# Feed-forward of a decoder trunk: two-by-two block products in seven multiplications, in two phases

## The chip, the cores and the metric

One NeuronCore of a Trainium2 chip runs one program, an inference step of a small decoder trunk. The metric is the device time of that program in microseconds (us), lower is better. Engines: TensorE (PE in the rows, PEld for its weight loads), VectorE (DVE), ScalarE (ACT), GpSimd (POOL), and SyncE (SP), whose queue issues the DMAs.

## What is computed

Two layers over 1088 tokens (1024 of a prompt, 64 of eight samples), 1024 features, fp32 in and out. Each layer is a mixer (layer 0: gating and pooling; layer 1: sliding-window attention), a cross-attention into 256 memory tokens, and the feed-forward, which alone is changed:

```python
D_FF = 2816
def conv_ffn(h, g_ctx, w_up, conv_w, conv_b, w_down):      # h = rmsnorm(x)
    T = h.shape[1]
    up = h @ w_up                                          # (T, 1024) x (1024, 5632)
    g, u = up[..., :D_FF], up[..., D_FF:]
    g_ext = jnp.concatenate([g_ctx, g], 1)
    gc = conv_b
    for j in range(3):
        gc = gc + conv_w[j] * g_ext[:, j:j + T]            # causal, over tokens
    y = (gelu(gc) * u) @ w_down                            # (T, 2816) x (2816, 1024)
    return y, g_ext[:, -2:]                                # x += y
```

## The kernel before, in words

Activations lie feature-major: a tile has 128 features on its partitions and tokens along its columns. The tokens go in three chunks, `CHS`, of 384, 384 and 320 columns. Each fp32 operand is split exactly into two float32r parts, high and low, and each product is three matmuls into one PSUM accumulation (`mm3`, L222 to L225): high x high, high x low, low x high. The residual stream is held as such parts, `xh` and `xl`, for the whole program; so are three staging tiles (`stage`, L103) and five weight tiles (`wtile`, L106), so that weights of the next part of the program are loaded while the last one computes. TensorE's order is the order of the program text (`manual_schedule`); the other engines' queues, and SyncE's, are put in an order by the scheduler, and each works in order.

`mem(l)` (L674) is the cross-attention. Its last part multiplies with `m_w_o` chunk by chunk and calls `x_update` (L267): VectorE adds PSUM to `xh`, GpSimd adds `xl`, and `split_x` (L254) splits the sum again and adds its square to `acc`, from which `norm_chunk` makes the RMS factors of each token and `spread` (L315) puts them along the columns (`rv`).

`ffn(l, last)` (L914) runs over 22 blocks `hb` of 128 hidden features. `gu(hb)` loads and splits a gate and an up weight of 1024 x 128 (`load_cols`, the gain folded in by GpSimd, L195; high part by ScalarE, L197; low part by GpSimd, L198). Per chunk: `proj_fm`, 8 x 3 matmuls for the gate (L227); VectorE times `rv` (L945); the convolution as one ScalarE and two VectorE operations (L956 to L958); GELU (L961); GpSimd times `rv` (L966); 24 matmuls for up; VectorE product (L968); split of the result into `h` (L296, L297). `down(i)` takes two blocks: for each of eight output blocks and each chunk six matmuls (L985) and one VectorE add from PSUM onto the running residual `x32` (L992). Up and down alternate: `gu(2i)`, `down(i-1)`, `gu(2i+1)`. In the last `down` of layer 0 each finished block is split again into `xh`/`xl` at once; in the last `down` of layer 1 each finished chunk is transposed and stored (`final`, L1000).

## Time and profile before

| | |
|---|---|
| median of 3 runs | 2722.21 us (2721.33 to 2723.23) |
| span of the profiled execution | 2719.6 us |
| TensorE busy | 2652.5 us, 98% of the span |
| VectorE busy | 1642.5 us, 60% |
| ScalarE busy | 915.0 us, 34% |
| GpSimd busy | 1062.7 us, 39% |
| mean granted TensorE clock | 0.987 of full |

The page of a profile lists the busy time of each engine, the span in slices, the DMA queues, the chain of work that ended last, and groups of equal instructions. Further views answer for a stretch: busy time by engine in windows, instructions in order of time, waits. Matmul durations are pipelined: a row's 0.33 us is the time from issue to the last result, and what a matmul costs in a stream is the distance between two starts.

### The profile page before, as it was taken

To read this page: it belongs to the slowest core of one execution; us is meant where nothing else is said; L and a number is where in the kernel's file an instruction comes from. 1 tells how busy PE (TensorE), PEld (TensorE's weight loads), DVE (VectorE), ACT (ScalarE), POOL (GpSimd) and SP (SyncE) were. 2 spreads that over 40 slices of the span, in tenths; PEclk is the share of its full clock that TensorE was granted. 3 is DMA by queue.
4 is the path that set the end of the run, shared out by engine and by line. 5 is a ranking of instruction groups with operands and counts; after the bars stand their busy time and mean duration, and the time that the engine had idled before them with its cause. 6 is when DMAs were issued, how large, how long until landed. Compare 5 with 4: busy or idle time off the path is not lost.

```text
span 2719.6 us, 39268 instructions
## 1 busy us (share of the span) xinstructions
PE 2652.5 (98%) x15552; PEld 2469.7 (91%) x15552; DVE 1642.5 (60%) x3286; ACT 915.0 (34%) x1903; POOL 1062.7 (39%) x748
## 2 busy tenths in 40 slices
PE   8999999999999999999999989999999999999999
PEld 6998887899999999999876768877999999999999
DVE  8646965766555555554667677856665545555544
ACT  5224544332222222221545555553322222222221
POOL 3516533655333333331533333424663333333420
PEclk9999999999999999999999998999999999999999
DMA  8302102311111111110111021113111111111101
GB/s 268 113 11 69 47 32 86 101 47 40 47 40 47 47 47 47 40 47 24 58 37 46 1 63 47 47 40 117 55 39 47 47 47 47 47 40 47 47 24 69
DMA packets 167798, 150.49 MB, mean 55 GB/s; under 512 B 6465, under 2 KB 132511, under 8 KB 167614
## 3 DMA queue, kind: packets, MB, share of 16 engines
q1 hardware_dynamic: 167614, 147.98, 17.6%
q8 instruction: 122, 2.00, 0.3%
q14 instruction: 62, 0.51, 0.1%
HBM read 136.06 MB, written 11.82 MB: 54 GB/s over the span
## 4 chain that ended last, share of the span: by engine, by line
PE 83%; DVE 9%; POOL 2%; ACT 2%; issue 2%; DMA 0%; SPq 0%; ACTq 0%; DVEq 0%; POOLq 0%
PE psa L223 18%; PE psa L224 18%; PE psa L225 18%; PE psb L223 6%; PE psb L225 6%; PE psb L224 6%; DVE s L297 3%; PE psb L128 2%; PE psb L746 1%; PE psb L771 1%; PE psb L807 1%; DVE xl L257 1%; DVE w L219 1%; PE psa L128 1%; PE psa L1202 1%
## 5 line engine op out<-in xcount | busy, mean ns | idle before, releaser
L223 PE MATMUL psa<-xh,w 128*128 128x384 f32 (+1 forms) x2304 | 752.8, 327 | 5.1 <-DVE gp L945 5.1
L225 PE MATMUL psa<-xh,w 128*128 128x384 f32 (+1 forms) x2304 | 751.6, 326 | 0.0
L224 PE MATMUL psa<-xl,w 128*128 128x384 f32 (+1 forms) x2304 | 751.1, 326 | 0.0
L198 POOL TENSOR_TENSOR w<-st,w 128x1024 fp32r<-128x1024 f32 x140 | 343.2, 2454 | 419.4 <-ACT w L197 411.4
L223 PEld LDWEIGHTS psa<-xh,w 128*128 128x128 f32 x2304 | 433.0, 188 | 6.2 <-DVE gp L945 5.7
L224 PEld LDWEIGHTS psa<-xl,w 128*128 128x128 f32 x2304 | 433.1, 188 | 0.0
L225 PEld LDWEIGHTS psa<-xh,w 128*128 128x128 f32 x2304 | 432.9, 188 | 0.0
L223 PE MATMUL psb<-h,w 128*128 128x384 f32 (+1 forms) x1056 | 348.6, 330 | 2.6 <-DVE x L992 2.5
L225 PE MATMUL psb<-h,w 128*128 128x384 f32 (+1 forms) x1056 | 347.1, 329 | 0.0
L224 PE MATMUL psb<-h,w 128*128 128x384 f32 (+1 forms) x1056 | 346.9, 329 | 0.0
L197 ACT ACTIVATE w<-st 128x1024 fp32r<-128x1024 f32 x164 | 172.8, 1057 | 503.6 <-PE psb L225 362.8
L992 DVE TENSOR_TENSOR x<-psb,x 128x384 f32<-128x384 f32 (+1 forms) x480 | 251.1, 532 | 148.4 <-PE psb L225 147.0
L966 POOL TENSOR_TENSOR t<-t,rv 128x384 f32<-128x384 f32 x132 | 127.6, 966 | 353.7 <-ACT t L961 284.6
L195 POOL TENSOR_TENSOR st<-st,vec 128x1024 f32<-128x1024 f32 x84 | 166.1, 1977 | 205.8 <-DMA st<-in_f_w_up_dram 135.3
L968 DVE TENSOR_TENSOR t<-t,psa 128x384 f32<-128x384 f32 x132 | 70.1, 531 | 239.2 <-POOL t L966 239.2
L224 PE MATMUL psa<-s,w 128*128 128x384 f32 (+1 forms) x576 | 197.5, 343 | 16.5 <-DVE s L297 15.8
L223 PE MATMUL psa<-s,w 128*128 128x384 f32 (+1 forms) x576 | 197.8, 343 | 6.1 <-ACT s L296 6.0
L223 PEld LDWEIGHTS psb<-h,w 128*128 128x128 f32 x1056 | 198.2, 188 | 5.3 <-DVE x L992 5.0
L225 PEld LDWEIGHTS psb<-h,w 128*128 128x128 f32 x1056 | 198.3, 188 | 0.0
L224 PEld LDWEIGHTS psb<-h,w 128*128 128x128 f32 x1056 | 198.3, 188 | 0.0
L225 PE MATMUL psa<-s,w 128*128 128x384 f32 (+1 forms) x576 | 194.1, 337 | 0.0
L223 PE MATMUL psa<-w,xh 128*128 128x512 f32 (+1 forms) x432 | 180.1, 417 | 0.0
(289 smaller groups left out, 4332.9 us busy)
## 6 DMA issues: line engine op xcount, KB each, us to landing
st<-in_f_w_up_dram SPq DMA_DIRECT2D x88, 512.0 KB
st<-in_f_w_down_dram SPq DMA_DIRECT2D x44, 512.0 KB
ks<-in_m_w_kv_dram SPq DMA_DIRECT2D x16, 512.0 KB
st<-in_cache_mem_k_dram SPq DMA_DIRECT2D x16, 512.0 KB
k<-in_cache_mem_v_dram SPq DMA_DIRECT2D x16, 512.0 KB
st<-in_ab_w_in_dram SPq DMA_DIRECT2D x12, 512.0 KB
st<-in_c_w_qkv_dram SPq DMA_DIRECT2D x12, 512.0 KB
ks<-in_x_prompt_dram SPq DMA_DIRECT2D x8, 512.0 KB
```

The lines of the kernel that those rows point to most:

```text
L128: T.transpose(out, in_, idt[:rows, :rows])
L195: (eng or P).tensor_tensor(out=v, in0=v, in1=gain.unsqueeze(2).to_broadcast([128, shape[0], shape[1]]), op=ALU.mult)
L197: S.activation(w[:, 0, :], st, AF.Copy)
L198: (eng or P).tensor_tensor(out=w[:, 1, :], in0=st, in1=f(w[:, 0, :]), op=ALU.subtract)
L219: V.scalar_tensor_tensor(out=w[:, 1, k, :], in0=sk, scalar=gk, in1=f(w[:, 0, k, :]), op0=ALU.mult, op1=ALU.subtract)
L223: mm(out, lhsT=ah, rhs=bh, start=first, stop=False)
L224: mm(out, lhsT=ah, rhs=bl, start=False, stop=False)
L225: mm(out, lhsT=al, rhs=bh, start=False, stop=last)
L297: V.tensor_tensor(out=t[:, 1, :src_n], in0=src, in1=f(t[:, 0, :src_n]), op=ALU.subtract)
L966: P.tensor_tensor(out=ge[:, :n], in0=ge[:, :n], in1=rv[c], op=ALU.mult)
L968: V.tensor_tensor(out=ge[:, :n], in0=ge[:, :n], in1=pu[:, :n], op=ALU.mult)
L992: V.tensor_tensor(out=xm, in0=ps[:, :n], in1=xm, op=ALU.add)
```

## The change

The feed-forward's products are made as two-by-two block products with seven multiplications in place of eight (the form with shared sums, in which the second, third and fourth results build on partial sums of the first). The tokens go in two halves of 544 (`HT`), each half in two quarters of 272 (`QT`); the weights go in blocks of 256 output features and two halves of the inner dimension.

- `combos_w` loads two weight pieces and makes seven left operands, four of them from sums on GpSimd; ScalarE and VectorE split each into two parts. `combos_b` makes seven right operands of a token half, sums and low parts all on VectorE.
- `seven` walks over jobs. A job is seven products of 3 x `nk` matmuls of 272 columns; its order is 1, 7 of the job before, 5, 6, 4 of the job before, 2, 3. Products 6, 7 and 4 go on accumulating in the bank of product 1, product 3 in that of product 5, and each partial result is read out in between.
- All of up comes first. The right operands `B` of both token halves are made at the start, from the normalised residual, and stay. The gated rows go to DRAM (`hd`). Then all of down, in segments of 6, 6, 6 and 4 blocks: rows are read back, combined (`load_b`), and each of the seven results of a job is added to `x32`.
- The residual leaves the chip at the end of `mem` (`xq` in DRAM) and is read back into `x32` for down. `xh`, `xl`, `stage`, `wtile` and `tmp` are no longer held over the feed-forward: their pools are closed and opened again behind it, and the residual is split anew (`after_ffn`). The last tiles are transposed and stored behind the last job (`final`).

The diff, cut to its core:

```diff
-    def x_update(c, m, ps):
+    def x_update(c, m, ps, xq=None):
...
-        split_x(c, m, t1)
+        if xq is None:
+            split_x(c, m, t1)
+            return
+        squares(c, m, t1)
+        o = CHS[c][0]
+        for q in range(2):
+            a, b = max(o, HT * q), min(o + n, HT * q + HT)
+            if a < b:
+                nc.sync.dma_start(out=xq[q][:, m, a - HT * q:b - HT * q], in_=t1[:, a - o:b - o])
...
+    def seven(jobs):
...
+            pa_ = psA()
+            prod(job, pa_, "1", True)
+            out("m1", pa_[:, :QT])
+            last("7")
+            pc_ = psB()
+            prod(job, pc_, "5", True)
+            out("m5", pc_[:, :QT])
+            prod(job, pa_, "6", False)
+            out("u2", pa_[:, :QT])
+            last("4")
+            pb_ = psB()
+            prod(job, pb_, "2", True)
+            out("m2", pb_[:, :QT])
+            prod(job, pc_, "3", False)
+            out("m53", pc_[:, :QT])
...
+    def combos_w(pl, src1, src2, nk, engs):
...
+        def split(i, src):
+            t = pl.tile([128, 2, nk, 128], F32R, tag="w", name="w", bufs=R["wbufs"])
+            S.activation(t[:, 0], src, AF.Copy)
+            engs[i].tensor_tensor(out=t[:, 1], in0=src, in1=f(t[:, 0]), op=ALU.subtract)
+            w[i] = t
...
+        split("1", a11)
+        s1 = comb(a21, a22, ALU.add)
+        split("5", s1)
+        s2 = comb(s1, a11, ALU.subtract)
+        split("6", s2)
+        split("2", a12)
+        split("3", comb(a12, s2, ALU.subtract))
+        split("7", comb(a11, a21, ALU.subtract))
+        split("4", a22)
...
+    def combos_b(pl, tl, x, j0, nj, b, engs):
...
+            S.activation(t[:, 0, j0:j0 + nj], src, AF.Copy)
+            engs[i].tensor_tensor(out=t[:, 1, j0:j0 + nj], in0=src, in1=f(t[:, 0, j0:j0 + nj]), op=ALU.subtract)
...
+        split("1", x11)
+        t1 = comb(x12, x11)
+        split("5", t1)
+        t2 = comb(x22, t1)
+        split("6", t2)
+        split("2", x21)
+        split("3", x22)
+        comb(x22, x12, x12)
+        split("7", x12)
+        split("4", comb(x21, t2))
...
+    def ffn(l, last, xq, rvq, rs):
...
+            R["wbufs"] = 10
+            wpl = es.enter_context(pool(f"fw{l}"))
+            bq = es.enter_context(pool(f"fb{l}"))
+            B = [{i: bq.tile([128, 2, 4, QT], F32R, name=f"b{q}{i}") for i in "1562374"} for q in range(2)]
+            with ExitStack() as ee:
+                ep = ee.enter_context(pool(f"fe{l}"))
+                for q in range(2):
+                    for j in range(0, 4, 2):
+                        hx = ep.tile([128, 2, 2, HT], F32, tag="hx", name="hx")
+                        for kh in range(2):
+                            nc.sync.dma_start(out=hx[:, kh], in_=xq[q][:, 4 * kh + j:4 * kh + j + 2, :])
+                        for kh in range(2):
+                            for i in range(2):
+                                kb = 4 * kh + j + i
+                                V.scalar_tensor_tensor(out=hx[:, kh, i], in0=hx[:, kh, i], scalar=g_ffn[l][:, kb:kb + 1],
+                                                       in1=rvq[:, HT * q:HT * q + HT], op0=ALU.mult, op1=ALU.mult)
+                        combos_b(None, ep, hx, j, 2, B[q], ident)
...
+            def load_b(s, q):
+                nk = SEGS[s] // 2
+                hx = ep.tile([128, 2, nk, HT], F32, tag="hx", name="hx")
+                for kh in range(2):
+                    nc.sync.dma_start(out=hx[:, kh], in_=hd[s][:, kh, :, HT * q:HT * q + HT])
+                b = {i: bq.tile([128, 2, nk, QT], F32R, tag="b", name="b", bufs=14) for i in "1562374"}
+                combos_b(None, ep, hx, 0, nk, b, ident)
+                return b
...
+            def down_out(mp, q):
+                def add(i, nh, ps):
+                    x = x32[q][:, 2 * mp + i, QT * nh:QT * nh + QT]
+                    V.tensor_tensor(out=x, in0=ps, in1=x, op=ALU.add)
...
-        mix0(mem_kv())
-        mem(0)
-        ffn(0, False)
-        swa()
-        mem(1)
-        ffn(1, True)
+        with ExitStack() as rs:
+            with ExitStack() as es:
+                open_main(es, 0)
+                mix0(mem_kv())
+                xq, rvq = mem(0, rs)
+            x32, conv_out = ffn(0, False, xq, rvq, rs)
+            with ExitStack() as es:
+                open_main(es, 1)
+                after_ffn(0, x32, conv_out)
+                rs.close()
+                swa()
+                xq, rvq = mem(1, rs)
+            x32, conv_out = ffn(1, True, xq, rvq, rs)
+            final(x32, conv_out)
```

Readout of a result: in a gate job of up, ScalarE copies three partial results and VectorE makes three sums, then the convolution runs over 544 columns; in an up job VectorE makes the sums, GpSimd (VectorE for one of four) multiplies with the gate, and SyncE's queue stores the rows.

## Rows read from the trace of the kernel before

**Rows 1.** The page: busy time, share of the span and instructions of each engine.

```profile
PE 2652.5 (98%) x15552; PEld 2469.7 (91%) x15552; DVE 1642.5 (60%) x3286; ACT 915.0 (34%) x1903; POOL 1062.7 (39%) x748
```

**Rows 2.** Windows of both feed-forwards and the tail: busy us, granted clock, DMA share, GB/s.

```profile
523.90:1321.50 797.60, 792.26 (x4782) 788.50 (x4782) 447.50 (x801) 202.53 (x340) 319.38 (x211) 1.00 0.15 44
1912.30:2711.80 799.50, 796.34 (x4831) 795.27 (x4831) 434.75 (x785) 184.07 (x298) 299.11 (x193) 1.00 0.15 45
2711.80:2719.60 7.80, 2.66 (x24) 2.33 (x22) 2.56 (x4) 1.78 (x3) 0.00 (x0) 1.00 0.50 173
```

**Rows 3.** The same view, a stretch in the middle of layer 0's feed-forward.

```profile
700.00:900.00 200.00, 200.00 (x1214) 199.96 (x1213) 106.50 (x194) 46.92 (x77) 73.26 (x44) 1.00 0.15 45
```

**Rows 4.** Timeline, TensorE: start, duration, instruction; widths 384 and 320.

```profile
800.17 0.33 PE L223 MATMUL psa<-xh,w 128*128 128x384 f32 x1
...
801.03 0.33 PE L225 MATMUL psa<-xh,w 128*128 128x384 f32 x1
...
2708.70 0.31 PE L224 MATMUL psb<-h,w 128*128 128x320 f32 x1
...
2709.29 0.31 PE L225 MATMUL psb<-h,w 128*128 128x320 f32 x1
```

**Rows 5.** Timeline, weight loads of six matmuls with two columns each.

```profile
516.03 0.78 PEld L283 LDWEIGHTS psb<-ones,acc 128*128 128x128 f32 x6
```

**Rows 6.** Chain that ended last (a load of 0.5 MB), and windows of 10 to 20 us.

```profile
1373.83 3.69 DMA st<-in_c_w_qkv_dram
...
10.00:20.00 10.00, 10.00 (x42) 8.36 (x42) 9.46 (x18) 7.26 (x13) 1.55 (x2) 1.00 1.03 391
```

**Rows 7.** Timeline, VectorE's convolution steps without a wait for GpSimd.

```profile
807.04 0.62 DVE L958 SCALAR_TENSOR_TENSOR t<-gp,vec,t 128x384 f32<-128x384 f32 x1
...
816.73 0.57 DVE L958 SCALAR_TENSOR_TENSOR t<-gp,vec,t 128x336 f32<-128x336 f32 x1
```

**Rows 8.** Timeline, VectorE, instructions that follow each other.

```profile
812.72 0.42 DVE L948 TENSOR_TENSOR gp<-psa,rv 128x256 f32<-128x256 f32 x1 [1.68 <-PE psa L225]
813.06 0.21 DVE L951 TENSOR_TENSOR gp<-psa,rv 128x64 f32<-128x64 f32 x1
...
1320.60 0.54 DVE L257 TENSOR_TENSOR xl<-x,xh 128x384 fp32r<-128x384 f32 x1
1321.06 0.55 DVE L265 TENSOR_TENSOR acc<-acc,t 128x384 f32<-128x384 f32 x1
1321.53 0.48 DVE L992 TENSOR_TENSOR x<-psb,x 128x320 f32<-128x320 f32 x1
1321.93 0.83 DVE L257 TENSOR_TENSOR xl<-x,xh 128x384 fp32r<-128x384 f32 x1
```

**Rows 9.** Windows around an idle stretch of TensorE.

```profile
1891.20:1893.40 2.20, 0.14 (x2) 0.04 (x1) 1.59 (x4) 1.39 (x4) 2.20 (x3) 1.00 0.00 0
1893.80:1900.40 6.60, 5.32 (x20) 5.28 (x21) 4.20 (x7) 1.84 (x6) 2.28 (x3) 0.50 0.01 4
```

**Rows 10.** Groups by line and form: GpSimd and ScalarE; busy, mean ns | idle before.

```profile
L966 POOL TENSOR_TENSOR t<-t,rv 128x384 f32<-128x384 f32 x88 | 88.9, 1010 | 284.6 <-ACT t L961 284.6
L966 POOL TENSOR_TENSOR t<-t,rv 128x320 f32<-128x320 f32 x44 | 38.7, 879 | 69.0 <-ACT t L964 69.0
L296 ACT ACTIVATE h<-t 128x384 fp32r<-128x384 f32 x88 | 46.2, 525 | 201.4 <-DVE t L968 201.4
```

**Rows 11.** Timeline, VectorE and GpSimd at the same time.

```profile
814.43 2.26 DVE L957 SCALAR_TENSOR_TENSOR t<-gp,vec,t 128x336 f32<-128x336 f32 x1 [0.94 <-ACT t L956]
819.35 0.55 DVE L992 TENSOR_TENSOR x<-psb,x 128x384 f32<-128x384 f32 x1
...
813.92 2.41 POOL L198 TENSOR_TENSOR w<-st,w 128x1024 fp32r<-128x1024 f32 x1 [4.62 <-ACT w L197]
818.98 2.41 POOL L198 TENSOR_TENSOR w<-st,w 128x1024 fp32r<-128x1024 f32 x1
```

**Rows 12.** Timeline, TensorE at the end: the transposes of the last chunk.

```profile
2711.64 2.82 PE L128 MATMUL psb<-idt,x 128*128 128x128 f32 x24
```

More of the change, by code (lines that the diff above doesn't have):

```diff
@@ L23 @@
 NT = 9
+HT = 544
+QT = 272
+SEGS = [6, 6, 6, 4]
 NEG = -1.0e30
@@ L893, in mem @@
                     norm_chunk(j // 2 - 1)
+                    factors(j // 2 - 1)
                 if hf == 0 and c:
```

415 lines of the change are left out of this document (284 added, 131 removed).

## Prediction

> **What bounds the kernel now.** I read the page's busy times first: TensorE is busy 98% of the span, VectorE 60%, ScalarE 34%, GpSimd 39% [rows 1]. Then the stretches of the two feed-forwards: layer 0 from 523.9 to 1321.5 us, layer 1 from 1912.3 to 2711.8 us and a tail of 7.8 us to the span's end, 1604.9 us in all, with TensorE without a hole in the middle [rows 2, 3]. The reader is to see that nothing but TensorE's stream sets the time there. Third, the timeline, for what one matmul takes: five starts of 384 columns take 0.86 us, four of 320 columns 0.59 us [rows 4], 0.172 and 0.147 us each. Over the stretch of 200 us, 1214 matmuls of mean width 362.7 came, one per 0.1647 us [rows 3]. At the full clock (2.4 GHz) a column is 0.417 ns, so 384 columns are 0.160 us and 320 are 0.133: about 13 ns come on top of each matmul at either width.
>
> The Trainium skill, TensorE: Matmul & The Clock Gate, section "Back-to-back issue gap", gives N/2.4 + 2.5 ns when the clock is high. The trace does not agree: by that rule 384 columns would start every 162.5 ns and not every 0.17 us. By it the new matmul of 272 columns would take an estimated 115.8 ns, the matmuls of a layer 642 us, and the whole some 2627 us.
>
> **What the change does to TensorE.** Before, a layer has 44 x 3 x 24 = 3168 up matmuls and 11 x 8 x 3 x 2 x 3 = 1584 down matmuls, 4752, which at 0.1643 us (two of 384 at 0.173, which the mean over 200 us wants, to one of 320 at 0.147) are 781 us. After, a job is seven products of 3 nk matmuls of 272 columns: 44 up jobs with nk = 4 (3696 matmuls), 24 down jobs with nk = 3 and 8 with nk = 2 (1848), 5544 in all. One takes 113.3 + 13.2 = 126.5 ns, extrapolated from the two widths. Bounds: below, the weight loads, six of which go in 0.78 us with 0.19 us for the last, 0.118 us apart [rows 5]; above, the 320-column start, 0.147 us. I take 126.5 because two widths gave the same constant. That is 467.5 us up and 233.8 us down, 701.3 us: 79.5 us less per layer, 159 us in two. The question is what of it is given back.
>
> **Start of the up phase.** Before, the up matmuls take the next chunk at once. After, TensorE needs all seven right-hand combinations of a token half, and these are made from one tile `hx` with a single buffer, in four rounds (two halves, two k parts). By the shapes and the order of opening of the pools, `hx` lies some 185 to 194 KiB up, on the last `s3` tiles of mem(), which the last mem matmul reads (E): so it can't be loaded earlier. A round is
> - two loads, 1.11 MB: 3.7 us for the first half MB and 1.4 us for the rest at 391 GB/s, 5 us [rows 6];
> - four scalar_tensor_tensor of 544 columns, 0.70 us apart from 0.62 us at 384 and 0.57 at 336 [rows 7]: 2.8 us;
> - eleven VectorE operations of 544 columns. From start to start 384 columns take 0.46 to 0.47 us, and PSUM reads of 256 and 320 columns 0.34 and 0.40 us [rows 8]: 1.03 ns a column and 0.07 us, so 0.63 us here, 7.0 us.
>
> So 14.8 us a round, and the first combination of the second round is there after 5 + 2.8 + 1.4 = 9.2 us. With 2 us for the last residual and the issue, the first matmul starts at E + 26. Its first five products take 7.6 us, to E + 33.6; the second half's first product is ready at E + 2 + 3 x 14.8 + 9.2 = E + 55.6. Idle: 26 + 22 = 48 us a layer (bounds 36, where loads and the VectorE work overlap, and 65, where SyncE's queue puts residual stores and weights ahead of `hx`). The norm's matmuls and the weights' splits fit into these holes.
>
> After a hole the granted clock is at the lower level: 0.50, 1.2 GHz, over 6.6 us behind the nearly idle 2.2 us at 1891 us [rows 9]. At most half of such 6.6 us is lost each time; I take 2.5 us, three holes a layer, 7.5 us (0 to 10).
>
> **The up phase.** Per pair of blocks TensorE has 4 x 84 x 0.1265 = 42.5 us. VectorE: 14 splits of 512 columns at 0.60 (8.4 us), eight conv steps of 544 with the wait for the one before at 0.82 (6.6), evictions 5, small copies 2: 22 us. GpSimd: eight sums of 512 columns (1.26 us, between 0.88 at 320 and 1.01 at 384 and on with their slope of 2 ns a column) and six products at 0.78: 14.8 us [rows 10]. ScalarE: 14 splits at 0.63, 14 copies out of PSUM at 0.4 and 8 passes of the conv at 0.7 to 0.9: 21 us, scaled from 0.525 us at 384 [rows 10]. All below 42.5. What can hurt is the order: a bank is accumulated on again two products (3 us) after its copy was due, and VectorE and ScalarE work in order. VectorE with two SBUF inputs waits for a running GpSimd operation: 0.57 us of work took 2.26 us and ended 0.4 us behind GpSimd's, while an add from PSUM ran beside one in 0.55 us [rows 7, 11]. Stalls: 10 us a layer (0 to 40). The new stores of gated rows (1088 B a partition, four per up job) go through SyncE's queue, nearly free (DMA share 0.15 [rows 3]).
>
> **Down.** Per segment of six blocks TensorE has 8 x 63 x 0.1265 = 63.8 us. VectorE: 56 adds of 272 at 0.35 (19.5 us, one per product, where before one add closed six matmuls), 28 weight splits of 384 at 0.467 (13.1), 22 operations of 816 columns on the gated rows at 0.91 (20.0): 52.6 us. GpSimd: 16 sums of 384, 1.0 us each [rows 10]. About half of VectorE's time is of the kind that waits; with 0.4 us for each sum it is at 59 us, 93% of TensorE's. In the last segment (four blocks) it is 43 + 4 against 42.5 us, so above it. In that state, with two products (2.3 us) of slack, I take 18 us of stalls a layer (5 to 45).
>
> Its start: `hx` of this phase lies on right-hand tiles that the last up job still reads, so the first product begins some 7 us after up's end; then VectorE has, for three jobs, 20 us of combinations, 6.5 of weights, 7.3 of adds and 3 of waiting, 37 us against 24 on TensorE. Loss 7 + 13 = 20 us (12 to 30). The residual's 4.5 MB load (11.4 us at that rate) comes at the same time.
>
> **Ends.** Layer 0: splitting the residual again was interleaved with the last down group and now follows it, but the first token half is final two jobs earlier: 5 us. Layer 1: nine tiles are transposed and stored behind the last job, where before only the last chunk's 24 transposes (2.82 us) and its stores stood there [rows 12]. 4.5 MB at 391 GB/s are 11.4 us, with 2.5 us ahead and 2 us behind: 16 us. mem()'s updates lose a copy and a subtraction: -1 us a layer.
>
> **Sum.** Layer 0: 48 + 7.5 + 467.5 + 10 + 20 + 233.8 + 18 + 5 = 809.8 us, before 797.6. Layer 1: with 16 for 5, 820.8 us, before 799.5 + 7.8 = 807.3. Together +25.7, less 2 for mem(): +24 us. The profiled execution has a span of 2719.6 us, the median of the runs is 2722.2, so 2746 us.
>
> **Rivals.**
> 1. Faster: the engines keep up, and only the holes remain. Start 42 + 5, up stalls 3, down's start 14, down stalls 8, ends 5 and 14: 778 and 787 us, 40 us less than before: 2681. For it: every engine's sum is below TensorE's in up and in the large segments. Against: the last segment's sum isn't, and 1.14 us per down product leaves no room for two 816-column operations in a row.
> 2. Slower by the shared port: VectorE's down phase sets the end. If each GpSimd sum holds VectorE for its whole length, a segment takes 52.6 + 16 = 68.6 us and the last one 55: 261 us, with in-order waits 274, and up's stalls grow to 25: 37 us more a layer, 2820. It decides as soon as more than 0.7 us of each 1.0 us sum blocks VectorE in down. For it: the row of 2.26 us. Against: adds from PSUM run beside GpSimd, and are half of the instructions [rows 11]. The Trainium skill, SBUF — State Buffer, section "SBUF: two separate sides", says just this: VectorE with two SBUF inputs against a GpSimd operation is an exclusive lock for the whole instruction. By that rule the time is this rival's; the trace agrees for single instructions and cannot show how often they meet.
> 3. The matmul is cheaper or dearer than 126.5 ns: at 118 ns, the weight load's, 654 us of matmuls a layer and 2652 in all; at 147 ns 815 us and some 2970. Two widths on one line speak against both.
>
> **How the numbers follow.** A measurement tells about 0.2% (5.4 us) from no change. Forecast 0.37 for 2728 to 2790; between it and rival 1, within 5.4 us of before, 0.10; rival 1 0.33; rival 2 0.17; rival 3 0.03 (0.02 below, 0.01 above). So faster 0.35, same 0.10, slower 0.55. The range 2665 to 2825 takes in the forecast, most of rivals 1 and 2 and no more.
>
> **What would show it.** Right: TensorE starts 0.126 to 0.127 us apart in mid-phase; two holes of 20 to 28 us at each start of up, VectorE busy in them; in down VectorE over 85% and TensorE waiting for its adds. Wrong: the second half's hole missing (then `hx` does not serialize), starts at 0.12 or 0.147, or GpSimd at the head of VectorE's waits over all of up. The least sure terms are the holes and the down stalls; if either is half of what I took, the sign turns.

## The result, and the profile after

The changed kernel takes 2822.3 us (median of 4 runs, 2818.13 to 2824.95), the kernel before 2721.8 beside it: ratio 1.037, 95% interval 1.0355 to 1.0385. The profiled execution has a span of 2823.2 us, 103.6 more than before. The prediction said 2746: the sign was right, the loss was four times as large.

The page of the changed kernel: busy time, share and instructions of each engine, and the granted clock in 40 slices, in tenths of 2.4 GHz. It answers [rows 1].

```profile
PE 2534.6 (90%) x17136; PEld 2336.3 (83%) x17136; DVE 1899.0 (67%) x3798; ACT 1190.9 (42%) x2483; POOL 983.5 (35%) x856
...
PEclk9999999779999997999899988999599999989999
```

TensorE has 118 us less to do and waits for 289 us instead of 67. Where it waits, windows of the changed kernel say: up and down of layer 0, the 11 us behind it, up and down of layer 1, the tail. Columns as in [rows 2]: TensorE, weight loads, VectorE, ScalarE, GpSimd, clock, DMA share, GB/s.

```profile
533.90:1066.00 532.10, 475.94 (x3709) 473.30 (x3708) 329.58 (x618) 230.23 (x427) 198.93 (x182) 0.94 0.24 76
1066.00:1357.10 291.10, 250.25 (x1854) 245.99 (x1853) 238.81 (x425) 97.57 (x169) 70.60 (x64) 0.91 0.29 100
1357.10:1368.10 11.00, 0.35 (x4) 0.09 (x2) 7.30 (x10) 11.00 (x28) 10.14 (x14) 0.57 0.50 161
1981.00:2515.80 534.80, 476.69 (x3709) 474.03 (x3708) 333.33 (x618) 230.05 (x427) 196.89 (x182) 0.93 0.24 76
2515.80:2805.20 289.40, 247.81 (x1852) 243.43 (x1852) 239.12 (x424) 97.47 (x168) 71.79 (x64) 0.92 0.29 100
2805.20:2823.20 18.00, 9.19 (x76) 7.99 (x74) 8.26 (x27) 5.86 (x10) 0.00 (x0) 0.90 0.70 260
```

The middle of up, the same 200 us as [rows 3]:

```profile
700.00:900.00 200.00, 200.00 (x1588) 200.00 (x1588) 121.48 (x235) 90.12 (x170) 81.57 (x78) 1.00 0.25 81
```

Three matmuls of 272 columns there, in the timeline, which answer [rows 4]:

```profile
700.08 0.29 PE L964 MATMUL psb<-b,w 128*128 128x272 f32 x1
700.21 0.29 PE L962 MATMUL psb<-b,w 128*128 128x272 f32 x1
700.34 0.29 PE L963 MATMUL psb<-b,w 128*128 128x272 f32 x1
```

200 us by 1588 is 125.9 ns a matmul, against 126.5 in the prediction, and TensorE waits for nothing there. The rule that the prediction cited from the Trainium skill (TensorE: Matmul & The Clock Gate, "Back-to-back issue gap"), which that section gives for a matmul by itself and not for a stream with weight loads, makes an estimated 115.8 ns; the trace doesn't agree.

So the gain on TensorE is there, and the loss lies at the joints. From the starts of the 5544 matmuls of 272 columns of a layer I read how long each stretch took, and by how much each job was longer than its matmuls (counted off as 84 a job in up, 63 or 42 in down):

| stretch, us | predicted, layer 0 / 1 | measured, layer 0 / 1 |
|---|---|---|
| end of mem(), against before | -1 / -1 | +10.0 / +9.0 |
| last product of mem() to the end of up | 533 / 533 | 532.3 / 534.9 |
| up's last to down's first product | 7 / 7 | 9.0 / 9.0 |
| first four jobs of down, over their matmuls | 13 / 13 | 24.5 / 25 |
| three segment boundaries of down | 18 / 18 | 24.8 / 22.7 |
| behind the feed-forward (layer 0: against before; layer 1: the whole tail, 7.8 before) | 5 / 16 | 24.3 / 18.3 |

The 24.3 us are read at the 800th matmul behind down's last: 179.3 us after it, against 155.0 in the kernel before. Up came out as forecast; the terms around it did not. What TensorE waited for longest (whole span; us, times, longest):

```profile
PE psa L962 <- ACT m L1152: 59.5, 2, 30.7
PE psa L962 <- DVE x L1253: 50.0, 24, 5.8
PE psa L962 <- ACT b L1037: 23.7, 2, 11.9
PE psb L344 <- DVE dg L343: 18.3, 12, 3.7
```

### The profile page after: what moved, and what is told of

The parts are those of the page before. It is cut to its first block, busy times and chain, and to the rows that moved or that the text cites. A ratio compares the mean times of both kernels' runs of the same rounds, so it can differ in the third digit from the quotient of the medians.

```text
span 2823.2 us, 45209 instructions
## 1 busy us (share of the span) xinstructions
PE 2534.6 (90%) x17136; PEld 2336.3 (83%) x17136; DVE 1899.0 (67%) x3798; ACT 1190.9 (42%) x2483; POOL 983.5 (35%) x856
## 3 DMA queue, kind: packets, MB, share of 16 engines
q1 hardware_dynamic: 183358, 223.76, 24.3%
## 5 line engine op out<-in xcount | busy, mean ns | idle before, releaser
L962 PE MATMUL psa<-b,w 128*128 128x272 f32 x2112 | 623.2, 295 | 152.1 <-ACT m L1152 59.5
L964 PE MATMUL psa<-b,w 128*128 128x272 f32 x2112 | 619.1, 293 | 10.2 <-DVE w L1011 10.2
L963 PE MATMUL psa<-b,w 128*128 128x272 f32 x2112 | 618.4, 293 | 10.1 <-DVE b L1038 10.1
L962 PEld LDWEIGHTS psa<-b,w 128*128 128x128 f32 x2112 | 406.1, 192 | 160.7 <-ACT m L1152 60.2
L964 PE MATMUL psb<-b,w 128*128 128x272 f32 x1584 | 462.8, 292 | 8.6 <-DVE w L1011 8.6
L963 PE MATMUL psb<-b,w 128*128 128x272 f32 x1584 | 463.4, 293 | 2.5 <-DVE b L1038 2.5
L962 PE MATMUL psb<-b,w 128*128 128x272 f32 x1584 | 463.7, 293 | 0.0
L964 PEld LDWEIGHTS psa<-b,w 128*128 128x128 f32 x2112 | 406.2, 192 | 12.1 <-DVE w L1011 11.9
L963 PEld LDWEIGHTS psa<-b,w 128*128 128x128 f32 x2112 | 406.1, 192 | 10.7 <-DVE b L1038 10.7
L1016 POOL TENSOR_TENSOR sc<-st 128x512 f32<-128x512 f32 (+2 forms) x152 | 196.0, 1289 | 474.7 <-DMA st<-in_f_w_up_dram 202.3
L1011 DVE TENSOR_TENSOR w<-sc,w 128x512 fp32r<-128x512 f32 (+2 forms) x304 | 221.0, 728 | 151.4 <-ACT w L1010 150.8
L964 PEld LDWEIGHTS psb<-b,w 128*128 128x128 f32 x1584 | 304.2, 192 | 9.2 <-DVE w L1011 9.2
L963 PEld LDWEIGHTS psb<-b,w 128*128 128x128 f32 x1584 | 304.3, 192 | 3.1 <-DVE b L1038 3.1
L962 PEld LDWEIGHTS psb<-b,w 128*128 128x128 f32 x1584 | 305.1, 193 | 0.2
L1010 ACT ACTIVATE w<-sc 128x512 fp32r<-128x512 f32 (+2 forms) x304 | 173.4, 571 | 209.0 <-PE psa L964 144.0
L1010 ACT ACTIVATE w<-st 128x512 fp32r<-128x512 f32 (+2 forms) x228 | 130.0, 573 | 148.8 <-PE psb L964 107.3
L232 PE MATMUL psa<-w,xh 128*128 128x512 f32 (+1 forms) x432 | 180.8, 419 | 10.6 <-ACT w L227 10.6
L1011 DVE TENSOR_TENSOR w<-st,w 128x512 fp32r<-128x512 f32 (+2 forms) x228 | 167.6, 737 | 25.7 <-ACT w L1010 25.3
L1016 POOL TENSOR_TENSOR sc<-st,sc 128x512 f32<-128x512 f32 (+2 forms) x76 | 91.8, 1208 | 264.4 <-DVE w L1011 261.6
```

Source lines behind the costliest of these rows:

```text
L232: mm(out, lhsT=ah, rhs=bh, start=first, stop=False)
L962: mm(ps[:, :QT], lhsT=wt[:, 0, k, :], rhs=bt[:, 0, k, :], start=first and k == 0, stop=False, skip_group_check=True)
L963: mm(ps[:, :QT], lhsT=wt[:, 0, k, :], rhs=bt[:, 1, k, :], start=False, stop=False, skip_group_check=True)
L964: mm(ps[:, :QT], lhsT=wt[:, 1, k, :], rhs=bt[:, 0, k, :], start=False, stop=k == nk_of(j) - 1, skip_group_check=True)
L1010: S.activation(t[:, 0], src, AF.Copy)
L1011: engs[i].tensor_tensor(out=t[:, 1], in0=src, in1=f(t[:, 0]), op=ALU.subtract)
```

## The experiments

Where nothing else is said, the edit is on the changed kernel. Times are one run each, the last kernel's is the median of four. The kernel before, timed beside them, took 2717.6 to 2724.4 us, so single times within some 7 us of each other tell little; the stretches, read from each run's trace in both layers, tell more.

### The start of up

The first of these waits was not in the prediction. The second hole of up's start, TensorE and ScalarE of the changed kernel in order of time:

```profile
570.05 0.59 PE L963 MATMUL psb<-b,w 128*128 128x272 f32 x1 [0.69 <-DVE b L1038]
600.37 0.59 PE L962 MATMUL psa<-b,w 128*128 128x272 f32 x1 [28.81 <-ACT m L1152]
...
599.37 0.66 ACT L1037 ACTIVATE b<-tc 128x544 fp32r<-128x544 f32 x1 [3.16 <-DVE tc L1043]
599.94 0.38 ACT L1152 ACTIVATE m<-psa 128x272 f32<-128x272 f32 x1
600.21 0.39 ACT L1152 ACTIVATE m<-psb 128x272 f32<-128x272 f32 x1
```

TensorE has done products 1 and 5 of the first job by 571 us and needs their copies made before it accumulates on the bank. The copies come behind the last split of both token halves.

**Two buffers for `hx`.**

```diff
- hx = ep.tile([128, 2, 2, HT], F32, tag="hx", name="hx")
+ hx = ep.tile([128, 2, 2, HT], F32, tag="hx", name="hx", bufs=2)
```

> Edit: the tile of gated-norm input that the start of up works on (hx) gets two buffers instead of one, so that the load of a round runs beside the work on the round before. In the changed kernel the rounds start 20.0, 18.8 and 13.4 us apart and the load takes 4.3 us of each from issue to the first multiply. Theory (the rounds are serialized by the single buffer, as the prediction said): three loads of 4.3 us per layer disappear from the path, job 2 of up starts 63 us after the last matmul of mem() instead of 76, -13 us a layer, 2796 us. Rival (the rounds are set by VectorE and ScalarE taking turns over the splits, and the load hides behind the last splits anyway): at most -4 us a layer, 2814 or more.

2814.7 us. Job 2 of up (here and below its start is counted at the 85th matmul, behind the first 84) starts 71.1 and 71.6 us after mem()'s last product instead of 76.1 and 78.8, 5 and 7 us less: between the two, nearer the rival. The single buffer was a part of the start, not what it hung on.

**The gate's tiles beside the start's.** The pool of `m`, `g` and `ge` was opened when the start's pool was closed, on the same memory.

```diff
- R["wbufs"] = 10
+ R["wbufs"] = 8
+ gpp = es.enter_context(pool(f"fg{l}"))
  with ExitStack() as ee:
      ep = ee.enter_context(pool(f"fe{l}"))
...
- gpp = es.enter_context(pool(f"fg{l}"))
...
```

> Edit: the pool of the gate's tiles (copies m, gates g, ge) is opened before the pool of the start's tiles and so lies beside it and not on top of it; to make room, 8 weight tiles instead of 10 and 4 ge tiles instead of 5. Theory: the second hole at the start of up (29.2 us) is TensorE waiting for the copies of product 1 and 5 out of PSUM, which can't be written before the start's last split, because their tiles lie on its memory; now the whole first job (10.6 us at the full clock, twice that at the lower) runs while the second token half is prepared, and job 2 waits only for the first combination of the second half: it starts some 61 us after the last matmul of mem() instead of 76, -14 us a layer, 2794 us. Rival (the prediction's: the second half's operand sets the second hole, and the first job is done by then): job 2 starts within 3 us of where it did, 2818 to 2826 us. Second rival: eight weight tiles stop TensorE in mid-phase, then steady jobs take over 10.7 us and the time is above 2822.

Job 2 starts at 62.4 and 63.5, up ends 13.5 and 15.2 us earlier: the copies waited for memory, as the theory said. What TensorE waits for now is the second token half's operands:

```profile
573.00 0.60 PE L962 MATMUL psa<-b,w 128*128 128x272 f32 x1 [6.50 <-ACT b L1037]
...
588.61 0.59 PE L962 MATMUL psa<-b,w 128*128 128x272 f32 x1 [11.49 <-ACT b L1037]
```

The second of these comes 56.4 us after mem()'s last product (57.5 in layer 1). The prediction had set 55.6 for the second half; that step was sound, and in the changed kernel the copies hid it.

But the time is 2819.6 us. The hole before down is 22.2 us instead of 9.0. SyncE's queue and VectorE in this run:

```profile
1056.17 0.82 SPq L1239 DMA_DIRECT2D x<-xq  x2
1057.08 1.85 SPq L1245 DMA_DIRECT2D hx<-hd  x2
...
1072.27 1.01 DVE L1043 TENSOR_TENSOR tc<-hx 128x816 f32<-128x816 f32 x1 [9.56 <-DMA hx<-hd]
```

The residual's 4.5 MB, now free to be issued early, went ahead of the gated rows: 15.2 us from issue to first use, against 5.0 in the changed kernel (issued at 1065.90, used at 1070.90).

### The hole before down

**Gated rows ahead of the residual**, the gate's tiles as above.

```diff
- for q in range(2):
-     nc.sync.dma_start(out=x32[q], in_=xq[q])
...
  b[q] = load_b(s, q)
+ if s == 0:
+     nc.sync.dma_start(out=x32[q], in_=xq[q])
```

> Edit: the gate's tiles beside the start's tiles, as before, and in down the load of the residual (4.5 MB) is issued behind the first load of gated rows instead of ahead of it. With the gate's tiles moved alone, up got 14 us shorter a layer and the wait between up and down grew from 9 to 22 us. Theory: that wait is the residual's transfer ahead of the gated rows in the queue; with the order turned the gated rows are there at up's end or before, and the hole is 5 us or less, so up's 14 us are kept and 4 us more are won: 2785 us. Rival (the hole is the memory of the operands or the weights' splits, whatever is loaded first): it stays at 15 us or more, 2805 or more.

2796.7 us: up's gain is kept, the hole is back at 10.4 and 9.9 us, and not at 5. The order explained what had been added, not what was there before.

**The gated-row tile on memory that is free earlier.**

```diff
- bq = es.enter_context(pool(f"db{l}"))
  ep = es.enter_context(pool(f"de{l}"))
+ bq = es.enter_context(pool(f"db{l}"))
```

> Edit: on top of the edit that turned the order of the residual's and the gated rows' loads (2797 us), the pool of down's gated-row tile is opened ahead of the operands' pool, so that it lies on up's operands of the first token half, which are read for the last time one job before up's end, and no longer on those of the second half, which the last product reads. Theory: the 10 us between up's last and down's first product are the load that can only be issued when that memory is free, then the load, then the first combinations; with the load 8 to 10 us earlier the hole is 3 us or less and the first four jobs lose 24 us or less over their matmuls as before: 2797 less 14 to 22, so 2775 to 2783. Rival (down's own operands and weights lie on tiles read until the end as well, so that VectorE can't begin earlier whatever is loaded): the hole stays at 8 us or more, 2793 or more.

2797.1 us, holes 10.7 and 10.8: the theory fell. The load was issued at 1052.41 us, when up ended, because it stood in SyncE's queue behind seven stores of gated rows that wait for up's last products.

**That load from ScalarE's queue.**

```diff
- nc.sync.dma_start(out=hx[:, kh], ...)
+ (S if s == 0 and q == 0 else nc.sync).dma_start(out=hx[:, kh], ...)
```

> Edit: on top of the kernel with the moved gated-row tile (2797 us), the very first load of gated rows in down is issued from ScalarE's queue and not from SyncE's, where it stood behind seven stores that wait for up's last products. Theory (SyncE's in-order queue holds the load until up's end): it is issued 8 us before up's last product, behind ScalarE's last copy, its 4.2 us lie under up, and the hole of 10.7 us before down's first product shrinks to 4 to 6 us (VectorE's first combination and ScalarE's first splits remain), 5 us a layer or more: 2783 to 2789 us. Rival (down's operand tiles lie on up's, which the last products read, so VectorE and ScalarE can't write before up's end): the load is early but the hole stays at 9 us or more, 2794 or more.

2792.1 us, holes 10.2 and 9.5. The gated rows were early; now the first weights of down were late. The queues of ScalarE and SyncE, then ScalarE's first split:

```profile
1043.34 0.92 ACTq L1242 DMA_DIRECT2D hx<-hd  x2
...
1041.69 9.52 SPq L1174 DMA_DIRECT2D hd<-m  x5
1051.30 0.96 SPq L1002 DMA_DIRECT2D st<-in_f_w_down_dram  x2
...
1055.78 0.52 ACT L1010 ACTIVATE w<-st 128x384 fp32r<-128x384 f32 x1 [12.04 <-DMA st<-in_f_w_down_dram]
```

The weights' loads stood behind the same stores. Neither explanation that I had put down held: the gated rows alone weren't it, and it wasn't operand memory, for with both loads out of SyncE's queue (the last run below) the hole is 3.1 us in either layer. That run also has the sums on VectorE; by themselves they left the hole at 9.0 and 8.9, so what they add to the queue's part isn't shown.

**Filling the hole**, to see what the lower clock costs.

```diff
...
+ for _ in seven(keep()):
      pass
+ pd = psB()
+ for _ in range(72):
+     mm(pd[:, :QT], lhsT=wlast[0]["1"][:, 0, 0, :], rhs=B[1]["1"][:, 0, 0, :], start=True, stop=True)
```

> Edit: the changed kernel with 72 matmuls of 272 columns added behind up's last product (9.1 us at 0.126 each), on operands that lie ready and into a bank that nobody reads, so that TensorE works through the hole before down and the granted clock has no reason to fall. Theory A (VectorE's preparation sets the first four jobs of down, which lose 24 us over their matmuls): the first product starts at most 1 us later, the clock is 1.00 in the first jobs, and they take 56 us as before: 2823 us, so the lower clock costs nothing there. Theory B (the first jobs are long because of the clock of 0.50, 24 and 10 us long in that stretch): the first four jobs lose 10 us less, 2803 us.

2854.4 us, and no answer: the residual's load had come ahead of the gated rows' (issues at 1069.74 and 1070.58 us), which were used at 1085.77, 15.2 us after their issue. With the residual held behind them:

> Edit: 72 idle matmuls behind up's last product, as in the earlier run that came out at 2854 us, now with the residual's load held behind the first load of gated rows, since in that run the scheduler had put the residual's 4.5 MB first and the gated rows landed 15 us after their issue. Theory A (VectorE's preparation sets the first four jobs of down): first product 9 to 10 us after up's last real product, first four jobs 54 to 57 us as without the idle matmuls (56.3), although the clock doesn't fall in the hole: 2820 to 2826 us. Theory B (the lower clock, 24 and 10 us long there, makes the first jobs long): first four jobs 46 us or less, 2805 or less. If the idle matmuls hold memory that the gated rows need, the first product comes later than 12 us after up's last and the run tells only about the clock by its window.

2827.6 us. Windows of this run: the hole filled with matmuls, the rest of the wait, and then to the end of down's fourth job:

```profile
1065.50:1074.60 9.10, 9.10 (x75) 9.07 (x73) 3.70 (x5) 1.78 (x2) 0.00 (x0) 1.00 0.88 321
1074.60:1080.20 5.60, 0.20 (x3) 0.01 (x1) 5.60 (x7) 4.50 (x6) 0.00 (x0) 0.83 0.99 384
1080.20:1129.60 49.40, 38.61 (x253) 37.37 (x254) 45.65 (x71) 19.00 (x34) 24.67 (x19) 0.81 0.49 175
```

The same in the changed kernel, the wait and the four jobs:

```profile
1066.00:1075.00 9.00, 0.28 (x4) 0.06 (x2) 4.45 (x6) 2.37 (x4) 0.00 (x0) 0.64 0.94 328
1075.00:1131.30 56.30, 41.39 (x253) 39.21 (x254) 51.14 (x76) 22.33 (x39) 22.89 (x18) 0.75 0.52 192
```

The first product came 14.7 us after up's end, later than the 12 us beyond which, by the expectation, the run tells of the clock only by its window. The fourth job ended 64.1 us after up's end, against 65.3, with a granted clock of 0.81 for 0.75 over the jobs. VectorE, busy 92% of those 49 us, is the likelier limit. But the order of the loads changed with the edit, and the clock fell again in the rest of the wait (a matmul every 0.23 us behind it), so that the lower clock costs nothing there isn't shown.

### Down: VectorE, and GpSimd's hold on it

A boundary in the changed kernel. TensorE, VectorE's queue ahead of the add that it waits for, and one sum of GpSimd's:

```profile
1171.66 0.56 PE L962 MATMUL psa<-b,w 128*128 128x272 f32 x1 [5.78 <-DVE x L1253]
...
1166.56 1.73 DVE L1038 TENSOR_TENSOR b<-tc,b 128x816 fp32r<-128x816 f32 x1
1168.21 0.55 DVE L1011 TENSOR_TENSOR w<-sc,w 128x384 fp32r<-128x384 f32 x1
1168.68 0.43 DVE L1253 TENSOR_TENSOR x<-psb,x 128x272 f32<-128x272 f32 x1
1169.03 1.67 DVE L1038 TENSOR_TENSOR b<-hx,b 128x816 fp32r<-128x816 f32 x1
1170.62 0.55 DVE L1011 TENSOR_TENSOR w<-st,w 128x384 fp32r<-128x384 f32 x1
1171.09 0.43 DVE L1253 TENSOR_TENSOR x<-psa,x 128x272 f32<-128x272 f32 x1
1171.44 0.99 DVE L1043 TENSOR_TENSOR tc<-hx,tc 128x816 f32<-128x816 f32 x1
...
1168.84 0.99 POOL L1016 TENSOR_TENSOR sc<-st 128x384 f32<-128x384 f32 x1 [1.41 <-DVE w L1011]
```

The add that frees the bank stands behind operations on the next segment's operands and weights; 816 columns take 0.99 us, or 1.67 to 1.73 beside GpSimd. The operation of 1169.03 us ends at 1170.70, 0.87 us behind GpSimd's sum; in this phase 39 of the 41 VectorE operations on SBUF (the on-chip memory of the tiles) that started beside a running sum ended 0.28 to 0.87 us behind it, by their width, while adds from PSUM took their 0.43 us beside one.

**Without the operands of segments 2 to 4.**

```diff
- b[q] = load_b(s, q)
+ if s == 0:
+     b0[q] = load_b(s, q)
+ b[q] = b0[q]
```

> Left out: the loading and the combinations of the gated rows of segments 2 to 4 of down; their products take the first segment's operands. Theory A (the stalls at the segment boundaries are VectorE's queue: 22 operations of 816 columns and 28 weight splits stand between the adds that free PSUM): the 10.5 us at each of the first two boundaries and the 5 us at the last disappear, down takes 258 us instead of 282 from first to last product, -22 us a layer, 2778 us. Theory B (they are VectorE held off by GpSimd's sums of the weights, which are still there): stalls stay wherever four jobs' new weights are made, -8 us a layer at most, 2806 or more.

2768.6 us. All three boundaries lose 0.0 us; down is 27.6 and 26.4 us shorter, the first four jobs lose 21 to 22 us still.

**Without the sums of weights on GpSimd.**

```diff
  def comb(x, y, op):
+     if nk < 4:
+         return y
```

> Left out: the sums of weight blocks in down (16 of 384 columns a segment on GpSimd); the splits take a block as it is, so GpSimd has no work in down. All splits, adds and combinations on VectorE stay. Theory A (VectorE's own queue): the 816-column operations beside GpSimd go from 1.75 back to 1.00 us, some four of them a boundary, so a boundary loses 7 to 8 us instead of 10.5: -9 us a layer, 2804 us. Theory B (GpSimd's lock is the cause, the prediction's second rival): no stall at the boundaries, -22 us a layer, 2778 us, and VectorE's add is no longer what TensorE waits for.

2792.8 us. The large boundaries lose 5.1 to 5.5 us instead of 9 to 10.5, the first four jobs 17; down is 18.0 and 16.1 us shorter. Between the two theories: without the sums about half of a boundary is left.

**The sums on VectorE**, nothing left out.

```diff
- ..., nk, engs)
+ ..., nk, {**engs, "+": V})
```

> Edit: the changed kernel with the 16 sums of weight blocks of a down segment on VectorE instead of GpSimd, nothing left out. Without the sums a boundary lost 5.4 us instead of 10.5 and the first four jobs 17 instead of 24. Theory A (GpSimd's hold on VectorE costs about what the sums cost on VectorE itself, 8 of them a boundary at 0.46 us, 3.7 us): a boundary loses 8 to 11 us, the total is within 8 us of 2823. Theory B (the hold is the main price and VectorE has room): boundaries lose 6 us or less, 2800 us. Theory C (VectorE is at its limit in the whole phase): boundaries over 13 us and steady jobs of down over 8.2 us, 2845 or more.

2811.5 us; large boundaries lose 7.7 to 8.8 us, down is 8.3 and 5.0 us shorter. The boundaries fit theory A, but for the least of them; the total is 3.5 us below its range, which one run can't tell from it. Windows of layer 0's down, first the changed kernel:

```profile
1075.00:1357.10 282.10, 249.97 (x1851) 245.93 (x1852) 234.36 (x420) 95.20 (x166) 70.60 (x64) 0.92 0.27 93
```

Without the sums:

```profile
1075.00:1339.30 264.30, 245.21 (x1849) 241.75 (x1850) 210.20 (x419) 93.27 (x166) 0.00 (x0) 0.95 0.29 100
```

With the sums on VectorE:

```profile
1077.00:1350.60 273.60, 247.16 (x1850) 242.12 (x1851) 236.29 (x484) 94.96 (x165) 0.00 (x0) 0.94 0.28 96
```

The same 420 VectorE instructions are busy 24.2 us longer when GpSimd makes 64 sums beside them, 0.38 us a sum; making the sums itself costs VectorE 26.1 us. GpSimd's help is worth nothing here: with the sums on VectorE down is 8 and 5 us shorter. The Trainium skill (SBUF — State Buffer, "SBUF: two separate sides") calls this an exclusive lock between the two engines for a whole instruction; the trace agrees, by the 39 of 41 operations above.

### The end of mem()

**The factors spread later.**

```diff
  norm_chunk(j // 2 - 1)
- factors(j // 2 - 1)
+ if j == 5:
+     factors(0)
...
+ factors(1)
  norm_chunk(2)
```

> Edit: in mem() the spread of a chunk's norm factors over the partitions (three pairs of matmuls behind a VectorE multiplication) no longer follows directly on the norm's own matmuls: chunk 0's comes 48 matmuls later, chunk 1's behind mem()'s last product. Theory: the 10 us that mem()'s tail grew by are TensorE waiting for VectorE and GpSimd between the two, twice 5 us, and the lower clock behind each; both go, mem() ends 8 to 10 us earlier in each layer, and the start of up, which waits for loads anyway, stays as long: 2803 us. Rival (the growth is the residual's store and the summing of squares on GpSimd, not the spread): mem() ends at most 2 us earlier, 2818 or more. Second rival: the time is given back, because the first multiplication of up's start waits for the factors: 2818 or more with mem() 8 us shorter and the start 8 us longer.

2805.6 us, mem(0) ends at 524.0, as in the kernel before (523.7), and the start is as long (76.2 and 76.9 us to job 2). What went, in the changed kernel: the spread waits behind the norm, whose result goes through VectorE, GpSimd and VectorE again, and the products behind run at 0.27 us each instead of 0.147 from 526 to 529 us. In the kernel before (first row below) the next product follows the norm's matmuls [rows 5] at once.

```profile
516.75 0.39 PE L223 MATMUL psa<-s,w 128*128 128x320 f32 x1
...
520.82 0.72 PE L304 MATMUL psb<-ones,acc 128*128 128x2 f32 x6
522.39 0.46 PE L344 MATMUL psb<-dg,ones 128*128 128x128 f32 x2 [0.85 <-DVE dg L343]
...
524.93 0.49 PE L344 MATMUL psb<-dg,ones 128*128 128x128 f32 x2 [0.95 <-DVE dg L343]
```

### Behind layer 0's feed-forward

The 40 us behind layer 0's feed-forward in the kernel before (columns as in [rows 2]), where TensorE is busy throughout, and the first products of the next layer in the changed kernel:

```profile
1321.50:1362.10 40.60, 40.60 (x204) 33.70 (x204) 20.38 (x65) 11.98 (x27) 19.09 (x26) 1.00 0.15 53
...
1368.06 0.80 PE L232 MATMUL psa<-w,xh 128*128 128x512 f32 x1 [10.65 <-ACT w L227]
1373.61 0.79 PE L233 MATMUL psa<-w,xh 128*128 128x512 f32 x1 [4.76 <-DVE w L228]
```

**Key and value weights first in program order** (`wkv` is made ahead of `after_ffn`).

> Edit: the second layer's first weights (key and value projection) are loaded and split ahead of the splitting of the residual behind the first feed-forward, in program order, instead of behind it. Theory: the 10.9 and 5.5 us in which TensorE waits there are ScalarE's and SyncE's order (the weights' splits stand behind 24 splits and 24 squares); the first product starts 5 to 6 us after the last one of the feed-forward and the second hole is under 2 us, -9 to -11 us, 2812 us. Rival (the load itself is late, because the tiles lie on memory of the down phase: loads can't start before its last product, and four MB-sized ones take until then): at most -3 us, 2819 or more.

2825.3 us, the 800th matmul at 179.1 us instead of 179.3: the rival. The loads went out at 1351.15 us, with down's last products (the last at 1352.4); their tiles lie on its memory.

**The weights loaded during down's third segment**, into tiles of their own, split first.

```diff
+ wk = rs.enter_context(tc.tile_pool(name="wk", bufs=1, reuse_waits="tile", side="right"))
+ R["wk"] = [wk.tile([128, 1024], F32, name=f"wk{r}") for r in range(4)]
...
```

> Edit: the four 0.5 MB loads of the second layer's key and value weights go into tiles of their own during down's third segment (to make room 14 weight tiles in down instead of 16 and 3 tiles of sums instead of 4), and their splits are first in program order behind down. With the splits first but the loads late, nothing had moved (TensorE waited for weights that landed 9 us after down's end). Theory (the loads are late because the staging tiles lie on down's memory until its last product; before the change they were loaded during the feed-forward): the first product starts 5 to 7 us after down's last instead of 11, no second hole over 3 us, 9 to 11 us less from down's end to the second mem()'s last product (624 us): 2812 us if down itself isn't slowed by fewer tiles. Rival (ScalarE's and VectorE's splits of residual and weights take that long whatever is loaded: 8 weight splits of 0.62 and 24 of the residual at 0.41 on ScalarE are 15 us): 3 us less at most, 2819 or more.

2826.5 us. The first product comes 6.2 us after down's last and not 11.4; by the 28th matmul 2 of these 5 us are left, at the 800th none (180.2): the rival again. TensorE waits for residual parts made on GpSimd:

```profile
1362.40 0.79 PE L233 MATMUL psa<-w,xh 128*128 128x512 f32 x1 [5.46 <-ACT xh L266]
...
1372.73 0.50 PE L235 MATMUL psa<-w,xl 128*128 128x512 f32 x1 [2.17 <-POOL xl L267]
1379.38 0.59 PE L305 MATMUL psb<-ones,acc 128*128 128x2 f32 x2 [5.47 <-POOL acc L279]
```

**The residual's splitting on VectorE alone**, with those early weights.

```diff
- split_x(c, m, x32[q][:, m, ...], True)
+ split_x(c, m, x32[q][:, m, ...], False, V)
```

> Edit: on top of the early key and value weights (2826 us), all subtractions and sums of squares of the residual's splitting behind layer 0's feed-forward are on VectorE; before, half of both were on GpSimd. With the early weights TensorE's first matmul came 5 us sooner, and by the 28th it had given them back waiting for GpSimd's subtractions, at the 76th it was where it had been (41 us behind down's last matmul, 17 in the kernel before). Theory (GpSimd, slow by itself and holding VectorE, sets that stretch): the 28th matmul comes at 15 us or less instead of 23, the 76th at 33 or less instead of 41, the 800th at 171 or less instead of 180: 2817 us. Rival (the sum of the work on ScalarE and VectorE sets it, whoever does it): 800th at 177 or more, 2823 or more.

2819.6 us; the 28th matmul at 16.2 us, the 76th at 35.3, the 800th at 174.8. Beside the early weights GpSimd was 5 us of it. The same 5 us went in the runs with the gated-row tile moved (2797.1 and 2792.1 us: 800th at 175.0 and 174.7), where GpSimd still makes half of the subtractions and the weights come late, and the last run, which has both edits, is at 174.7: the two don't add, and why the moved tile helps here was not looked into. Some 20 us against before stay in each of these runs. That they are the splitting, which before was interleaved with down's last group, is argued from the order of the work; no run interleaved it again.

### Together

**The first combination**: the gate's tiles beside the start's, gated rows ahead of the residual, the factors later, key and value weights first in program order, and `hx` in halves with two buffers.

> Edits together: the gate's tiles beside the start's, gated rows loaded ahead of the residual, the start's tile in halves with two buffers, factors spread later in mem(), key and value weights first. If the account of where the 100 us went is right and the parts add: 2823 less 28 (copies), 10 to 18 (hole before down), 10 (two buffers), 16 to 20 (mem), 10 (weights of the second layer): 2740 to 2750, the seven-multiplication kernel still no faster than the kernel before, because down's 48 us a layer over its matmuls and 50 us at the start of up stay. If the parts overlap (the same VectorE work at the start is what remains each time): 2765 or more.

2770.1 us: the parts overlapped. Job 2 of up still starts 62 to 64 us after mem(); from 525 to 588 us VectorE hardly rests (64 of the 68 us from 522 to 590).

**The second**: with the gated-row tile moved, and the very first sums on VectorE.

> All edits together (the gate's tiles beside the start's, the start's tile in halves with two buffers, factors spread later in mem(), key and value weights first, gated rows loaded ahead of the residual and into memory that is free earlier), and the sums of the very first weights of up and of down on VectorE instead of GpSimd. The combination without the last two edits gave 2770 us. If the hole before down is the place of the gated-row tile (8 us a layer) and GpSimd's hold at both starts costs another 6 to 8 us a layer: 2738 to 2745. If the start's VectorE work is all that counts there: 2755 or more. The kernel before is at 2722, and neither reaches it.

2767.0 us, holes of 10.7 us, job 2 at 62.3: the mem() and up terms had been won, and with the moved tile some 4 us behind layer 0 (800th at 175.8), but nothing at the hole, and nothing at up's start by the moved sums.

**The last**: the gate's tiles, the factors, the gated rows moved in memory, order and queue, down's first weights from ScalarE's queue as well, the sums of down and of the gate's weights in up on VectorE, the early key and value weights, and the splitting on VectorE alone; `hx` is whole again.

> All edits that the runs found useful, in one kernel: the gate's tiles beside the start's, the factors spread later, gated rows first and into early free memory, the first gated rows and down's first weights loaded from ScalarE's queue, sums of the gate's weights of up and of all weights of down on VectorE, key and value weights early, the residual's splitting on VectorE alone. If the parts add to the 2792 of the kernel with the first three of them (all but the late factors): 17 for the factors, 12 for the sums, 5 to 10 a layer for the hole before down, 5 to 9 for the residual: 2740 to 2748, ratio to the kernel before 1.007 to 1.011, still slower. If removing one wait uncovers the next each time, as at the hole before down: 2760 or more. Faster than the kernel before only if the start of up also shrank, which none of the edits does beyond 14 us a layer: under 2720 would refute the account.

2740.2 us against 2721.5 before, ratio 1.0077, interval 1.006 to 1.0094. It is 82 us faster than the change as made and slower than the kernel before. Down's two windows are the place to look:

```profile
1044.30:1315.00 270.70, 242.38 (x1850) 237.59 (x1849) 238.81 (x488) 97.87 (x168) 0.00 (x0) 0.96 0.32 107
...
2444.00:2717.90 273.90, 242.46 (x1850) 237.54 (x1849) 239.31 (x488) 97.47 (x168) 0.00 (x0) 0.96 0.29 98
```

From up's last to down's last product it is 20 and 15 us shorter than in the changed kernel. The hole gives 6 of them. The large boundaries lose 2.9 to 4.5 us, less than with the sums moved alone (7.7 to 8.8); why wasn't tried by itself. What is left, over matmuls of 126.5 ns: 54 us a layer in up, nearly all at its start, 37 and 40 in down with the hole before it, 20 behind layer 0's feed-forward against before, and a tail of 19.

## Why the prediction was right, and where it failed

The forecast was 24 us more than before, and 100.5 came. The direction was right, and so were the matmul's price and the sum for up. What failed are costs at the joints: the first four jobs of down (13 us set, 24.5 measured) and its stalls (18 set, 24.8 and 22.7 measured), the end of layer 0 (5 set, 24.3 measured), and mem() (-1 a layer set, +10 and +9 measured).

- **The matmul, 126.5 ns.** Right, 125.9. Two widths on one line were enough.
- **Start of up, 48 + 7.5 + 10 us.** The sum was right (532 and 535 us to up's end, forecast 533), its parts weren't. The first operands of the second round were there when forecast (560.13 us, 26.4 after mem()). The second half's operand came at 56.4 us, for 55.6 forecast, once the copies were moved. But in the changed kernel the second hole was the copies' memory, which the sum did not have, and not that operand; and in mid-phase there were no stalls at all (no job over 10.6 us); the 10 us set down for them paid for the longer hole. That was luck.
- **Down's start, 20 us.** The step failed by 13. The hole is 9 and not 7, and the first four jobs lose 24.5 and not 13. Counting VectorE's work was the right view (it is busy 51 of the 56 us), but the 3 us set down for waiting on GpSimd were too few: GpSimd makes 18 sums in the four jobs, and without the sums they lose 17, 7 to 8 us less. The other 4 us over the forecast were not taken apart.
- **Stalls in down, 18 us.** Sized by VectorE's average load (59 of 64 us a segment), measured 24.8 and 22.7. The 0.4 us per sum was right (0.38). What failed is the average: the work comes in a lump, since the operand tiles of a segment only come free in its last two jobs, and it loses 9 to 10 us at a large boundary and nothing that shows in the jobs between.
- **The second rival (GpSimd's hold)** named a true mechanism, but needed over 0.7 us a sum and got 0.38. 18 and 16 us a layer come back in down when the sums go, those of the forecast included, and the stalls that it had in up did not come. That its 2820 lies 2 us from the measured 2822 is an accident: it had neither mem() nor layer 0's end.
- **Behind layer 0, 5 us.** The largest miss, 19 us. I costed a delay of the splitting. The text that moved the splitting behind down also moved the loading of the next weights there, since their tiles were opened anew on down's memory; taking that away (the early weights) showed a wait for the splits and sums of squares behind it, as long. Of the 24 us, 5 went in runs; the cause of the rest is argued, not shown.
- **mem(), -1 us a layer.** Costed by the copy and the subtraction that go; the factors' spread, which comes directly behind the norm instead of one stretch later, costs 10 and 9; moving it later gave both back. Of a step that is moved I had not looked at what stood between it and its input before.
- **The clock, 7.5 us.** In up it can't be told from the waits that it lies in, and the run that filled the hole before down doesn't separate it either. It stays open.

Down by 19 and 17 us, the stretch behind layer 0 by 19 and the two ends of mem() by 21 make 76 of the 80 us missed. Each lies at a joint, where the prediction's steps for the middle of a phase don't hold.

## What to carry to other kernels

Where a phase is closed and the next opened on its memory, write down for each first tile of the next what it lies on and who reads that last, and for each first load which stores stand ahead of it in its queue; taking one such wait away uncovers the next (22, 10, 10, 10, 3 us here). Size a stall from the work that becomes possible at one moment, not from an engine's average load. Work that was interleaved can cost its whole length when it is moved to a joint (some 20 us here, by argument), and what was loaded during it is loaded after it.

## What was not expected of the hardware

VectorE's 420 instructions of a down phase were busy 234.4 us with 64 GpSimd sums beside them and 210.2 without, and 236.3 when VectorE made the sums too. A load of 1.7 MB was first used 5.0 us after its issue, and 15.2 us when 4.5 MB had been issued just before it on the same queue (1057.08 to 1072.27 and 1070.58 to 1085.77 us), with the DMA engines busy 0.97 of the time in the wait (1076 to 1090 us of that second run). A VectorE operation on SBUF that started beside a running GpSimd sum ended nearly its own whole length behind it (39 of 41 in layer 0's down), and an add from PSUM didn't wait (0.43 us).
